# Where the operands of TensorE begin in SBUF: all tiles on multiples of 256 bytes, and some weights up to 252 bytes behind that

## The chip, the cores and the metric

The kernel runs on one core of one Trainium2 chip. The metric is the device time of one execution in microseconds, as the median of several runs. Lower is better. The profile is of one execution of the same program.

## The reference

One layer of a hybrid encoder block on 1024 tokens with a model width of 1024, in float32:

```
h = x + 0.5 * SwiGLU_1(RMSNorm(x))                      # D_FF = 2816
u = RMSNorm(h);  [q|k|v|g_ret|p|gates] = u @ w_in       # 7 x 1024 columns
ret  = retention(rotary(q), rotary(k), v)  (4 heads, chunks of 64), head norm, * silu(g_ret)
pool = multiscale_pool(p)  (windows 2, 4, 8, 16), per-group matrix, scale
h = h + (sigmoid(gate_0) * (ret @ w_ret_up) + sigmoid(gate_1) * (pool @ w_pool_up)) @ w_out
h = h + 0.5 * SwiGLU_2(RMSNorm(h))
out = RMSNorm(h)
```

## The kernel before, in words

**Arithmetic.** Every float32 operand of a matrix product is split into a high part, rounded by ScalarE to the type `F32R`, and a low part, the rest, which VectorE subtracts (`split`, lines 150 to 152). One product of a 128x128 block of weights with a moving operand of 512 (or 256) columns is three matmuls, issued by `mm3` (lines 169 to 173): high weights by high operand (L171), high weights by low operand (L172), low weights by high operand (L173). Each matmul brings its own load of 128x128 weights, which the profile shows under PEld.

**Tiles.** A tile of weights (`wt`, tag `wt`, 5 buffers) holds four blocks of 128 columns, first the high and then the low parts: 4096 bytes in each partition, so that a block is 512 bytes. A tile of a moving operand (`mv`, 28 buffers) holds 512 columns high and 512 low: also 4096 bytes. The other kinds are `t4` (results and some operands, 9 buffers), `raw` (weights as they come from memory, 4), `tl` (4) and `c2` (512 columns in one part, 2048 bytes, 8 buffers).

**Products.** `strassen` makes a pair of output tiles from seven products, each of four blocks, so twelve matmuls of 512 columns, with weights that `prep_w` makes by `weights(t[n], ...)`. Two such groups that share operands take some of their products a level deeper: `common` makes seven products of 256 columns, two blocks each, so 42 matmuls, from four tiles of weights (`wx`, `ws12`, `ws34`, `wy`). There are 43 calls of `common`, in both SwiGLU input stages and in the projection. The output stages of the two SwiGLUs are in `ffn_out`: there a `step` loads a tile of weights and one moving operand, and makes twelve matmuls of 512 columns; 77 steps in the first SwiGLU and 66 in the second, whose last product (`near`, `far`) is written another way round. Moving operands of the 256-column products are halves of `mv` tiles, or differences that `Next.blocks` puts into buffers of tag `tl` or `t4`.

**Order.** The order of the instructions on each engine is written out by the kernel: `Flow.run` issues the preparation of a step four steps ahead of its matmuls, and puts pieces of other work between (`flow.rate` pieces a step).

**Where tiles begin.** Tiles lie one behind the other in each partition. Ahead of them stand 1152 bytes of the program's own, then `vec` and `neg` (256 each), `cst` (1344), `warm` (which takes 32), `zero` (1024) and `ones_r` (512): the tiles of tags `t4` and `raw` begin at byte 4576 and follow each other by 4096 bytes. 4576 is 17 x 256 + 224, so all of these lie 224 bytes behind a multiple of 256. Then come two tiles of 32 bytes (tag `ss`), so that `wt`, `mv`, `tl` and `c2`, which follow, all begin 32 bytes behind a multiple of 256. A block of weights (512 bytes), a low part (2048 bytes) and a half of an operand (1024 bytes) begin at whole multiples of 256 from the start of their tile. So the operands of nearly all matmuls begin 32 bytes behind a multiple of 256, both the weights and the moving operand; the exceptions are those where one of the two is a tile of tag `t4`, 224 bytes behind it: in retention, the masked scores `sm` as weights (`inner`, output `ob`) and the state as moving operand (`across`, output `xb`); in the SwiGLU input stages, two of the three differences of R22 (`y3`, `y4`) as moving operands.

Of the kernel before, what the change touches and what calls it, by code (L numbers as in the profile page):

```python
# [3 lines left out]

# [1 line left out]

# [4 lines left out]
F32 = mybir.dt.float32  # L11
F32R = mybir.dt.float32r
BF16 = mybir.dt.bfloat16
# [4 lines left out]
P = 128  # L18
S = 1024
D = 1024  # L20
KT = D // P
H = S // 2
# [24 lines left out]
LOG_DECAY = np.log(1.0 - 2.0 ** (-5.0 - np.arange(NH, dtype=np.float64)))  # L47

N_PS, N_SUM, N_IDLE = 6, 2, 6
N_MV, N_T4, N_RAW, N_WT, N_TL, N_C2 = 28, 9, 4, 5, 4, 8  # L50
LOOK = 4

# [37 lines left out]
def block_kernel(ctx: ExitStack, tc, x, x_tok, vecs, f1_in, f1_out, w_in, w_v, pool_w, w_ret, w_pool, w_o,  # L90
# [5 lines left out]
    act = nc.scalar.activation  # L96
    copy = nc.scalar.copy
    soon = tc.high_priority
    flow = Flow()

    cp = ctx.enter_context(tc.tile_pool(name="cp", bufs=1))
    sb = ctx.enter_context(tc.tile_pool(name="sb", bufs=1))
# [4 lines left out]
    def mv(name):  # L107
        return sb.tile([P, 2, H], F32R, tag="mv", bufs=N_MV, name=name)

    def wt(name):  # L110
        return sb.tile([P, 2, 4, P], F32R, tag="wt", bufs=N_WT, name=name)


    def raw(name):
# [7 lines left out]

    def c2(name):
        return sb.tile([P, H], F32, tag="c2", bufs=N_C2, name=name)

    def bank(name):
        return ps.tile([P, H], F32, tag="ps", name=name)

    def sum_bank(name):

        return ps.tile([P, H], F32, tag="sum", bufs=N_SUM, name=name)

    def load(dst, src):
        nc.sync.dma_start(dst, src)
# [7 lines left out]
    LO, HI = slice(0, HD), slice(HD, H)  # L142
# [4 lines left out]
    def flat(w, j, n=4):  # L147
        return w[:, j, :n].rearrange("p a b -> p (a b)")

    def split(hi, lo, src):  # L150
        copy(hi, src)
        tt(lo, src, hi.bitcast(F32), SUB)  # L152
# [5 lines left out]
    def operand(src, name):  # L158
        m = mv(name)
        split(m[:, 0], m[:, 1], src)  # L160
        return m

    def weights(src, name):
        w = wt(name)
        n = src.shape[-1] // P
        split(flat(w, 0, n), flat(w, 1, n), src)
        return w

    def mm3(dst, w, m, start, stop):

        mm(dst, w[0], m[0], start=start, stop=False, skip_group_check=True)  # L171
        mm(dst, w[0], m[1], start=False, stop=False, skip_group_check=True)  # L172
        mm(dst, w[1], m[0], start=False, stop=stop, skip_group_check=True)  # L173

    def parts(m, at=slice(None)):
        return m[:, 0, at], m[:, 1, at]
# [7 lines left out]
    nc.vector.memset(warm, 1.0)  # L184
    act(warm, warm, AF.Square)
    nc.vector.tensor_scalar(neg, vec, -1.0, None, MUL)
    zero = cp.tile([P, H], BF16, name="zero")
    nc.vector.memset(zero, 0.0)
    for n in range(N_SUM):
        b = sum_bank(f"set{n}")  # L190
# [2 lines left out]
            mm(b, zero[:, :P], zero, start=True, stop=True)  # L193
    ident, ones = cst[:, C_ID : C_ID + P], cst[:, C_ONE : C_ONE + P]
    ones_r = cp.tile([P, P], F32R, name="ones_r")


    def inverse_root(sums, n, name):
# [322 lines left out]
    def common(nx, A, B, n):  # L521

        src, to, which, R = ("L12", "a", (0, 0), "R21") if n == 2 else ("S4", "b", (0, 1), "R22")
        w, t, a, b = {}, {}, A.t, B.t

        def prep1():
            w["x"] = weights(a[src], f"{A.name}wx{n}")
            s = t["s"] = c2(f"{A.name}s12{n}")
            tt(s[:, LO], b[src][:, LO], b[src][:, HI], ADD)
            tt(s[:, HI], s[:, LO], a[src][:, LO], SUB)  # L530
            w["s12"] = weights(s, f"{A.name}ws12{n}")

        def prep2():

            s = a[src] if n == 3 else c2(f"{A.name}s34{n}")
            tt(s[:, LO], a[src][:, LO], b[src][:, LO], SUB)
            tt(s[:, HI], a[src][:, HI], t["s"][:, HI], SUB)
            w["s34"] = weights(s, f"{A.name}ws34{n}")

        def prep3():  # L540
            w["y"] = weights(b[src][:, HI], f"{A.name}wy{n}")

        def prod(dst, k, at, m, start=False):
            for z in range(2):
                mm3(dst, parts(w[k], at + z), nx.block(R, m, z), start and z == 0, z == 1)


        def one():
            x, y = (bank(f"{A.name}{k}{n}") for k in "xy")
            t["x"], t["A"], t["B"] = x, A.dest(which), B.dest(which)  # L550
            prod(x[:, LO], "x", 0, (0, 0), True)
            with soon():
                copy(t["A"][:, LO], x[:, LO])
            prod(y[:, HI], "s12", 0, "y1", True)
            with soon():
                copy(t["B"][:, HI], y[:, HI])
            prod(a[to][:, LO], "x", 2, (1, 0))

        def two():
            x = t["x"]  # L560
            prod(x[:, LO], "s12", 2, "y2")
            with soon():
                tt(t["A"][:, HI], x[:, LO], t["B"][:, HI], ADD)
            prod(a[to][:, HI], "s34", 2, (1, 1))
            with soon():
                A.finish[n]()

        def three():
            x = t["x"]
            prod(b[to][:, LO], "y", 0, "y4")  # L570
            prod(x[:, LO], "s34", 0, "y3")
            with soon():
                copy(t["B"][:, LO], x[:, LO])
                tt(t["B"][:, HI], x[:, LO], t["B"][:, HI], ADD)
                B.finish[n]()

        return [(prep1, one), (prep2, two), (prep3, three)]


# [215 lines left out]
    def ffn_out(ops, ready, w, res, name, sink, end, last=None):  # L795
# [67 lines left out]
        def step(n, f, k, where, start, after):  # L863
            o = {}

            def prep():
                L, X = f(k)
                o["w"] = weights(L, f"{name}{n}w{k}")
                o["m"] = operand(X, f"{name}{n}m{k}")

            def body():
                if start and k == 0:
                    for i in range(4):
                        bk[where, i] = (sum_bank if where == "b" and i < N_SUM else bank)(f"{name}{n}{where}{i}")
                for i in range(4):
                    mm3(bk[where, i], parts(o["w"], i), parts(o["m"]), start and k == 0, k == FH - 1)
                    if k == FH - 1:
                        after(i)

            return prep, body  # L880
# [65 lines left out]
        L, X = {}, {}  # L946
# [55 lines left out]
    load(cst, consts)  # L1002
    flow.add(lambda: copy(ones_r, ones))
    first.work(first.r11, first.r21, first.r12, first.r22, first.p22, first.t2, first.t3, first.t1, first.t4_)
    x_sums = sb.tile([P, 8], F32, tag="ss", bufs=2, name="x_sums")

    def x_square(t):
        r = tl(f"xs{t}")
# [351 lines left out]
    class Unit:  # L1360
# [5 lines left out]
        def loads(self):  # L1366
            await_stored(f"q{self.h}", f"k{self.h}", f"v{self.name}")
            at = slice(self.nh * H, (self.nh + 1) * H)
            self.src = {}
            r = self.src["v"] = tl(f"v{self.name}")  # L1370
            load(r, vs[self.h // 2 * 2 + self.nh][:, self.h % 2 * S : (self.h % 2 + 1) * S])
            for n, spilled in (("q", qs), ("k", ks)):
                r = self.src[n] = tl(f"{n}{self.name}")
                for i in range(2):
                    load(half(r, i), spilled[2 * self.h + i][:, at])
            if self.nh == 0:
                self.dec = sb.tile([P, H], F32, tag="dec", bufs=1, name=f"dec{self.h}")
                load(self.dec, decay[self.h])
                self.ss = sb.tile([P, 8], F32, tag="ss", bufs=2, name=f"ss{self.h}")
                self.O = {}  # L1380

        def follow(self, u):
# [188 lines left out]
    def after(nx):  # L1571

        def t2(i):
            nx.r22(i)
            nx.t2(i)

        return {0: nx.r11, 4: nx.r21, 1: t2, 3: nx.t3, 2: nx.t1, 6: nx.t4_, 5: nx.p22}
# [83 lines left out]
    class Last(Norm):  # L1661
# [15 lines left out]
        def turned(self, acc):  # L1677


            def gains():  # L1680
                self.row = sb.tile([P, S], F32, tag="mv", bufs=N_MV, name=f"{self.name}row")
                load(self.row, g_row)
                self.ssq_e = sb.tile([P, 8], F32, tag="ss", bufs=2, name=f"{self.name}sse")

            def done(n):

                o = self.rows[n] = sb.tile([P, S], F32, tag="mv", bufs=N_MV, name=f"{self.name}o{n}")
                b = self.turn([acc[mt] for mt in range(4)], n)
                act(half(o, 1), b, AF.Square, accum_out=self.ssq_e[:, n : n + 1])
                tt(half(o, 0), b, half(self.row, 0), MUL)  # L1690
                v = self.sums[n] = sb.tile([P, 8], F32, tag="st", bufs=10, name=f"{self.name}e{n}")[:, :1]
                nc.vector.tensor_scalar(v, self.ssq_e[:, n : n + 1], 1.0 / D, EPS, MUL, ADD)

            def rest(n):

                b = self.turn([acc[mt] for mt in range(4, 8)], n)
                if n < N_SUM:
                    self.banks[n] = sum_bank(f"{self.name}s{n}")
                    copy(self.banks[n], b)
                else:  # L1700
                    copy(half(self.rows[n], 1), b)

            return gains, *(lambda f=f, n=n: f(n) for n in range(4) for f in (done, rest))
# [144 lines left out]
```

## Time and profile before

| what | value |
|---|---|
| runs before | 2163.72, 2163.72, 2165.25 us; median 2163.72 us |
| profiled execution, first to last instruction | 2160.9 us |
| TensorE matmul busy | 2148.0 us, 10668 matmuls |
| weight loads busy | 1816.9 us |
| VectorE busy | 1870.0 us |
| ScalarE busy | 1088.9 us |
| granted TensorE clock | 0.999 of full speed |

The profiled execution's span is 2160.9 us, 2.8 us under the median of the timed runs; what lies between is around the first and the last instruction. A matmul's end is modelled in these records, and matmuls overlap: what one costs in a stream is the distance from its start to the start of the next, which the view of the work in order of time shows.

By the starts of the matmuls in the trace the span falls into these stages: the first SwiGLU's input products to about 430 us and its output products to about 640 us, projections and values to about 1170 us, retention and the pooling branch to about 1370 us, the merge and the output projection to about 1520 us, the second SwiGLU's input products to about 1940 us and its output products to the end.

### The profile page before, as it was taken

To read this page: it belongs to the slowest core of one execution; us is meant where nothing else is said; L and a number is where in the kernel's file an instruction comes from. 1 tells how busy PE (TensorE), PEld (TensorE's weight loads), DVE (VectorE), ACT (ScalarE), POOL (GpSimd) and SP (SyncE) were. 2 spreads that over 40 slices of the span, in tenths; PEclk is the share of its full clock that TensorE was granted. 3 is DMA by queue.
4 is the path that set the end of the run, shared out by engine and by line. 5 is a ranking of instruction groups with operands and counts; after the bars stand their busy time and mean duration, and the time that the engine had idled before them with its cause. 6 is when DMAs were issued, how large, how long until landed. Compare 5 with 4: busy or idle time off the path is not lost.

```text
span 2160.9 us, 29697 instructions
## 1 busy us (share of the span) xinstructions
PE 2148.0 (99%) x10668; PEld 1816.9 (84%) x10668; DVE 1870.0 (87%) x3300; ACT 1088.9 (50%) x2047; POOL 0.2 (0%) x4
## 2 busy tenths in 40 slices
PE   9999999999999999999999999999999999999998
PEld 7888888888888888888888898887888888888887
DVE  8799899998788798899767877899999989999784
ACT  8544444545656444444426754446644444455463
POOL 0000000000000000000000000000000000000000
PEclk9999999999999999999999999999999999999999
DMA  7232323596323333333485567624133232359532
GB/s 261 69 129 104 101 93 127 165 339 207 122 93 107 109 127 108 118 107 119 153 268 191 167 224 256 218 97 160 65 117 103 98 107 99 118 185 334 178 122 78
DMA packets 117828, 320.92 MB, mean 149 GB/s; under 512 B 12976, under 2 KB 17200, under 8 KB 117680
## 3 DMA queue, kind: packets, MB, share of 16 engines
q1 hardware_dynamic: 117104, 317.97, 43.4%
q8 instruction: 83, 1.36, 0.3%
q10 hardware_dynamic: 576, 1.05, 0.1%
q14 instruction: 65, 0.53, 0.1%
HBM read 228.27 MB, written 90.70 MB: 148 GB/s over the span
## 4 chain that ended last, share of the span: by engine, by line
PE 90%; DVE 7%; ACT 1%; issue 1%; DMA 1%; SPq 0%; ACTq 0%; DVEq 0%
PE c_b L171 2%; PE c_b L173 2%; PE c_b L172 2%; PE a_b L173 2%; PE a_b L171 2%; PE a_b L172 2%; PE c_e L173 2%; PE c_e L171 2%; PE c_e L172 2%; PE a_e L173 2%; PE a_e L171 1%; PE a_e L172 1%; PE bp6b L172 1%; PE bp6b L173 1%; PE bp6b L171 1%; PE c_a L172 1%
## 5 line engine op out<-in xcount | busy, mean ns | idle before, releaser
L172 PE MATMUL c_b<-n3T,c_wS 128*128 128x512 f32 x176 | 68.5, 389 | 0.0
L173 PE MATMUL c_b<-n3T,c_wS 128*128 128x512 f32 x176 | 68.5, 389 | 0.0
L171 PE MATMUL c_b<-n3T,c_wS 128*128 128x512 f32 x176 | 68.2, 390 | 0.0
L171 PE MATMUL a_b<-n1T,a_wS 128*128 128x512 f32 x168 | 65.5, 390 | 0.0
L172 PE MATMUL a_b<-n1T,a_wS 128*128 128x512 f32 x168 | 65.4, 389 | 0.0
L173 PE MATMUL a_b<-n1T,a_wS 128*128 128x512 f32 x168 | 65.4, 389 | 0.0
L173 PE MATMUL a_a<-n1R,a_wL 128*128 128x512 f32 x120 | 46.7, 390 | 0.8 <-DVE a_wL L152 0.8
L171 PE MATMUL a_a<-n1R,a_wL 128*128 128x512 f32 x120 | 46.8, 390 | 0.0
L172 PE MATMUL a_a<-n1R,a_wL 128*128 128x512 f32 x120 | 46.7, 389 | 0.0
L172 PE MATMUL c_a<-n3R,c_wL 128*128 128x512 f32 x112 | 43.7, 390 | 0.0
L171 PE MATMUL c_a<-n3R,c_wL 128*128 128x512 f32 x112 | 43.6, 389 | 0.0
L173 PE MATMUL c_a<-n3R,c_wL 128*128 128x512 f32 x112 | 43.6, 389 | 0.0
L173 PEld LDWEIGHTS c_b<-n3T,c_wS 128*128 128x128 f32 x176 | 33.0, 188 | 6.9
L171 PEld LDWEIGHTS c_b<-n3T,c_wS 128*128 128x128 f32 x176 | 33.0, 188 | 6.9
L172 PEld LDWEIGHTS c_b<-n3T,c_wS 128*128 128x128 f32 x176 | 33.0, 188 | 6.8
L171 PEld LDWEIGHTS a_b<-n1T,a_wS 128*128 128x128 f32 x168 | 31.5, 188 | 6.8 <-ACT a_v L471 0.3
L173 PEld LDWEIGHTS a_b<-n1T,a_wS 128*128 128x128 f32 x168 | 31.5, 188 | 6.6
L172 PEld LDWEIGHTS a_b<-n1T,a_wS 128*128 128x128 f32 x168 | 31.5, 188 | 6.5
L173 PE MATMUL c_e<-n3T,c_wS 128*128 128x512 f32 x88 | 35.1, 399 | 0.4 <-DVE c_wS L152 0.4
L171 PE MATMUL c_e<-n3T,c_wS 128*128 128x512 f32 x88 | 34.5, 393 | 0.0
L172 PE MATMUL c_e<-n3T,c_wS 128*128 128x512 f32 x88 | 34.4, 391 | 0.0
L173 PE MATMUL a_e<-n1T,a_wS 128*128 128x512 f32 x84 | 33.4, 398 | 0.9 <-DVE a_wS L152 0.9
(3058 smaller groups left out, 8076.2 us busy)
## 6 DMA issues: line engine op xcount, KB each, us to landing
c_ra<-in_f_in SPq DMA_DIRECT2D x22, 512.0 KB, 3.6
c_rb<-in_f_in SPq DMA_DIRECT2D x22, 512.0 KB, 4.1
a_ra<-in_f_in SPq DMA_DIRECT2D x21, 512.0 KB, 3.6
a_rb<-in_f_in SPq DMA_DIRECT2D x21, 512.0 KB, 4.4
t<-au SPq DMA_DIRECT2D x11, 512.0 KB, 2.6
b<-ag SPq DMA_DIRECT2D x11, 512.0 KB, 2.7
r<-au SPq DMA_DIRECT2D x11, 512.0 KB, 3.6
br<-r SPq DMA_DIRECT2D x11, 512.0 KB, 5.4
```

Source lines behind the costliest of these rows:

```text
L171: mm(dst, w[0], m[0], start=start, stop=False, skip_group_check=True)
L172: mm(dst, w[0], m[1], start=False, stop=False, skip_group_check=True)
L173: mm(dst, w[1], m[0], start=False, stop=stop, skip_group_check=True)
```

## The change

The instructions of each engine, their order and their waits stay as they are. What changes is where tiles begin. The tile `zero`, which the first twelve matmuls read, takes a buffer of tag `c2` and no longer room of its own, a tile of 32 bytes called `line` is put behind `ones_r`, and tiles of tag `ss` take 128 bytes: tags `c2`, `t4`, `raw`, `wt`, `mv` and `tl` now all begin on multiples of 256 bytes. A tile of weights is 256 bytes longer, and a caller of `weights` can put the weights `at` floats behind its start. Two callers do: `common`, where all four tiles of a call have the same place, and `step` in `ffn_out`. One running count `places` numbers the calls of both; the place is the count times 22 (in `common`) or 23 (in `ffn_out`), modulo 64, in floats: 0 to 252 bytes. All other weights keep place 0.

```diff
+LINE = 64
...
-    flow = Flow()
+    flow, places = Flow(), count()
...
-    def wt(name):
-        return sb.tile([P, 2, 4, P], F32R, tag="wt", bufs=N_WT, name=name)
+    def wt(name, at=0):
+        w = sb.tile([P, S + LINE], F32R, tag="wt", bufs=N_WT, name=name)
+        return w[:, at : at + S].rearrange("p (z i c) -> p z i c", z=2, i=4)
...
+    def eights(name):
+        return sb.tile([P, 32], F32, tag="ss", bufs=2, name=name)[:, :8]
...
-    def weights(src, name):
-        w = wt(name)
+    def weights(src, name, at=0):
+        w = wt(name, at)
...
-    zero = cp.tile([P, H], BF16, name="zero")
+    zero = sb.tile([P, 2 * H], BF16, tag="c2", bufs=N_C2, name="zero")[:, :H]
...
+    cp.tile([P, 8], F32, name="line")
...
     def common(nx, A, B, n):
...
+        at = next(places) * 22 % LINE
...
-            w["x"] = weights(a[src], f"{A.name}wx{n}")
+            w["x"] = weights(a[src], f"{A.name}wx{n}", at)
...
-            w["s12"] = weights(s, f"{A.name}ws12{n}")
+            w["s12"] = weights(s, f"{A.name}ws12{n}", at)
...
-            w["s34"] = weights(s, f"{A.name}ws34{n}")
+            w["s34"] = weights(s, f"{A.name}ws34{n}", at)
...
-            w["y"] = weights(b[src][:, HI], f"{A.name}wy{n}")
+            w["y"] = weights(b[src][:, HI], f"{A.name}wy{n}", at)
...
     def step(n, f, k, where, start, after):
...
-                o["w"] = weights(L, f"{name}{n}w{k}")
+                o["w"] = weights(L, f"{name}{n}w{k}", next(places) * 23 % LINE)
```

In the 1716 matmuls of the `ffn_out` steps about a quarter each of the weights begin in the first, second, third and fourth 64 bytes behind a multiple of 256. In the 1806 matmuls of `common` it is 546 in the first 64 bytes and 1260 in the other three.

More of the change, by code (lines that the diff above doesn't have):

```diff
@@ L2 @@
 from contextlib import ExitStack, contextmanager
-from itertools import chain
+from itertools import chain, count
 import numpy as np
@@ L1004, in block_kernel @@
     first.work(first.r11, first.r21, first.r12, first.r22, first.p22, first.t2, first.t3, first.t1, first.t4_)
-    x_sums = sb.tile([P, 8], F32, tag="ss", bufs=2, name="x_sums")
+    x_sums = eights("x_sums")
     def x_square(t):
@@ L1378, in loads @@
                 load(self.dec, decay[self.h])
-                self.ss = sb.tile([P, 8], F32, tag="ss", bufs=2, name=f"ss{self.h}")
+                self.ss = eights(f"ss{self.h}")
                 self.O = {}
@@ L1682, in gains @@
                 load(self.row, g_row)
-                self.ssq_e = sb.tile([P, 8], F32, tag="ss", bufs=2, name=f"{self.name}sse")
+                self.ssq_e = eights(f"{self.name}sse")
             def done(n):
```

## The prediction

> **What bounds the kernel now.** I read the page first: span, busy times and the chain of work that ended last.
>
> ```profile
> span 2160.9 us, 29697 instructions
> ...
> PE 2148.0 (99%) x10668; PEld 1816.9 (84%) x10668; DVE 1870.0 (87%) x3300; ACT 1088.9 (50%) x2047; POOL 0.2 (0%) x4
> ...
> PE 90%; DVE 7%; ACT 1%; issue 1%; DMA 1%; SPq 0%; ACTq 0%; DVEq 0%
> ```
>
> TensorE is busy for 99% of the span and makes 90% of the chain. So the time is the number of matmuls times their distance, and a change to where operands lie can matter only through that distance, or by making another engine late. Next I read the work in order of time, for the distance of matmuls of 512 columns, in a stretch where nothing waits (eleven rows, the first and the last shown), and for when a weight load starts beside them.
>
> ```profile
> 519.70 0.39 PE L172 MATMUL bp6b<-bp7m,bp7w 128*128 128x512 f32 x1
> ...
> 521.96 0.39 PE L173 MATMUL bp6b<-bp7m,bp7w 128*128 128x512 f32 x1
> ...
> 1520.00 0.39 PE L171 MATMUL wo3b<-mgR,wo3wS 128*128 128x512 f32 x1
> 1520.01 0.19 PEld L172 LDWEIGHTS wo3b<-mgR,wo3wS 128*128 128x128 f32 x1
> ```
>
> Ten steps take 2.26 us: about 226 ns each. The load of the next weights starts 0.01 us after a matmul starts, so both streams of reads begin together each time. The same view where retention goes from `st` to `ob`, matmuls of 256 columns:
>
> ```profile
> 1225.06 0.28 PE L172 MATMUL st<-v,kd 128*128 128x256 f32 x1
> ...
> 1225.66 0.28 PE L171 MATMUL ob<-v,sm 128*128 128x256 f32 x1
> ...
> 1226.00 0.28 PE L171 MATMUL ob<-v,sm 128*128 128x256 f32 x1
> ```
>
> Five steps of `st` take 0.60 us, 120 ns each; three of `ob` take 0.34 us, 113.3 ns each. These are the same kind of instruction on the same shape. What differs is the place: `st` has weights and moving operand both 32 bytes behind a multiple of 256, `ob` has weights of tag `t4`, at 224. The groups by line and shape repeat it (mean duration, which is the distance plus 163 ns in both cases):
>
> ```profile
> L172 PE MATMUL c_b<-n3T,c_wS 128*128 128x512 f32 x176 | 68.5, 389 | 0.0
> ...
> L172 PE MATMUL st<-v,kd 128*128 128x256 f32 x48 | 13.6, 283 | 0.0
> ...
> L172 PE MATMUL ob<-v,sm 128*128 128x256 f32 x48 | 13.2, 276 | 0.0
> ...
> L173 PE MATMUL c_x<-n3R22y,c_ws 128*128 128x256 f32 x40 | 11.2, 280 | 0.0
> ...
> L173 PE MATMUL c_x<-n3R21y,c_ws 128*128 128x256 f32 x32 | 9.1, 283 | 0.0
> ...
> L1505 PE MATMUL ot<-cst,o 128*128 128x128 f32 x64 | 7.6, 273 | 0.0
> ```
>
> Where both begin at 32 the duration is 283 (`st`, and `c_x` with R21's differences in `tl`); where one lies in `t4` it is 276 (`ob`), and it is 280 for `c_x` with R22, half of whose operands lie in `t4` and half in `tl`. So there is a price of about 6.7 ns a matmul for beginning at the same place modulo 256, and it is in the kernel's steady state: 389 less 163 is 226 for 512 columns.
>
> **How a distance is made up.** 512 columns take 226.7 and 256 take 120.0: 106.7 ns for 256 columns, and 13.3 ns beside them. In `ob` it is 6.7 beside them. 13.3 is twice 6.7, and 6.7 ns is what 16 columns take, 64 bytes of a partition. My reading: operands are read in pieces of 64 bytes. 512 floats that begin at 32 modulo 64 touch 33 pieces and not 32, one piece (6.7 ns) too many; 224 is 32 modulo 64 too, so `ob` has that too. And where the load of weights begins in the same 64 bytes of 256, both want the same part of the memory at once, and the matmul waits for one more piece. The first half of the reading is an inference; the second is what the rows show.
>
> **The change part by part.** Program counts: 8042 matmuls of 512 columns and 2334 of 256 in F32R, of 10668 records.
>
> (a) 6326 matmuls of 512 columns end with both operands at 0. Bounds: no gain (only the relative place counts, and it stays equal), and 13.3 ns (both parts go), below nothing too, see the rivals. I take 6.7, the piece that alignment takes away, since the collision of equal starts stays: 6326 x 6.7 = 42.2 us.
>
> (b) 1716 matmuls of the `ffn_out` steps. Three quarters (1287) begin in other 64 bytes than the operand: 6.7 to 13.3, taken at 10.0, since weights at odd places were not seen to be free: 12.9. The other quarter as in (a): 2.9. Together 15.7 us.
>
> (c) 1806 matmuls of `common`. In the two windows below the 42 of a call take 4.97 and 5.03 us, 119 ns each. After it 113.3 (the `ob` row) is the dear end; the cheap end is bound by the loads of weights, which in the transposes `ot` are what 128 columns wait for (duration 273, so 110 by the same 163). I take 112: 7 x 1806 = 12.7 us.
>
> (d) Retention: `st` and the scores, 240 of 256 columns, lose a piece, 1.6 us; `ob`, and `xb` like it, win a piece and get a collision, nothing.
>
> ```profile
> 125.00:500.00 375.00, 372.82 (x1919) 318.25 (x1920) 352.19 (x630) 179.01 (x327) 0.00 (x0) 1.00 0.44 149
> 1420.00:1500.00 80.00, 78.98 (x345) 64.24 (x344) 78.25 (x130) 46.94 (x83) 0.00 (x0) 1.00 0.39 132
> 1500.00:1920.00 420.00, 419.55 (x2188) 359.66 (x2188) 395.27 (x723) 209.50 (x389) 0.00 (x0) 1.00 0.31 107
> 1661.28:1666.31 5.03, 5.03 (x43) 5.03 (x42) 3.97 (x7) 3.12 (x6) 0.00 (x0) 1.00 0.66 201
> 1671.78:1676.75 4.97, 4.97 (x43) 4.96 (x42) 4.97 (x11) 3.04 (x6) 0.00 (x0) 1.00 0.02 3
> ...
> L152 DVE TENSOR_TENSOR c_wS<-c_S,c_wS 128x512 fp32r<-128x512 f32 x46 | 31.4, 685 | 1.2 <-ACT c_wS L151 1.2
> ...
> 1520.27 0.69 DVE L1629 TENSOR_TENSOR wo<-wo2b,wo 128x512 f32<-128x512 f32 x1
> 1520.87 0.69 DVE L257 TENSOR_TENSOR n3ssq<-n3ssq,n3q 128x512 f32<-128x512 f32 x1
> ```
>
> (e) What comes late next. The windows (columns: length, then busy time of PE, PEld, DVE, ACT, POOL) show VectorE at 352 of 375, 78 of 80 and 395 of 420 us in the stages with Strassen products. Those 4452 matmuls save about 30 us, which leaves VectorE 10 us of slack in each long stage and none at 1420 to 1500. It has more than busy time tells, since one operation shows 685 ns but the next starts 0.60 us after it. I let VectorE take back a third of the 30 us: 10 us. If it took all, 30.
>
> (f) Costed at nothing: writing weights at odd places, 143 tiles in `ffn_out` and 172 in `common`, two operations each, off TensorE's path while VectorE and ScalarE have slack; the VectorE rows at 32 and 224 are alike, but no row is at a place that is no multiple of 32. 630 operations dearer by one piece would be 4 us, hidden except in (e)'s stages. `zero` in a `c2` buffer adds no wait: its matmuls are over in the first 7 us. DMA is 1% of the chain.
>
> Sum: 42.2 + 15.7 + 12.7 + 1.6 - 10 = 62.2 us. The profiled execution's span is 2160.9 us; the median of the runs, 2163.7, is 2.8 more, which stays: 2098.7 and 2.8 are 2101.5, so 2101 us.
>
> **The rivals.**
>
> *Only the relative place counts.* The fixed 6.7 ns is not a piece too many but a cost of every such matmul. For it: no row here has a moving F32R operand on a multiple of 64. Then (a) is nothing; (b) 1287 x 6.7 = 8.6; (c) 546 at 120 and 1260 at about 115 (between `ob` and `c_x` with R22) against 119 now, 4.5; `ob` loses 144 x 6.7 = 1.0. 2163.7 - 12.1 = 2152 us.
>
> *The collision goes with the alignment.* With whole pieces the two streams interleave. For it: 13.3 is all there is to win. 8042 x 13.3 = 107 and 2334 x 10 = 23, of which VectorE takes back 30 or so, since its windows then bind: 100 less, 2064 us. The Trainium skill, "TensorE: Matmul & The Clock Gate", section "Back-to-back issue gap", has N / 2.4 + 2.5 ns for a warm matmul, 216 for 512 columns; the 226 here differ, and going by the page the gain would be 10.9 and not 13.3 ns on the 8042, an estimate near 2083.
>
> *Nothing moves.* Distances are set by something that goes with tags and not with addresses. Against it: `c_x` shows both durations for the same product with its operand in `t4` or `tl`. Time 2164 us. By the Trainium skill, the same page, section "Step-by-step: what each phase is for", TensorE has two independent read ports and loading the next weights takes nothing from the running matmul's reads; that would make this rival certain, and the rows `st` and `ob` disagree with it by 6.7 ns.
>
> *Slower: equal starts on whole pieces collide more.* At 32 the first piece of either stream is half used, which sets them apart after the first meeting; on 256 they would meet again at later pieces, in all 6326 matmuls of (a). The trace has dearer matmuls of the same shape and place, up to 397 against 389:
>
> ```profile
> L173 PE MATMUL c_b<-n3T,c_wS x176: 387/389/397, 1534.3 to 1928.6; 128*128 128x512 f32 x176
> ```
>
> At 8 ns each that is 51 us, with the rest unmoved: 2214 us. It decides from 4.6 ns a matmul on, where it eats up (b) and (c) with 28 us. Against it: the 226 are steady, a fixed price and not repeated ones.
>
> **How the numbers follow.** Forecast (equal starts collide, alignment saves one piece) 0.50, own range 2085 to 2125 by (b) and (e); relative place alone 0.12 (2152); collision gone 0.12 (2064); nothing moves 0.08 (2164); slower 0.18 (2168 to 2214). The range from 2064 to 2168 leaves out the slower case. A difference of 0.2%, 4.3 us, is about what a measurement of this kernel can tell from none. Faster by more: 0.50 + 0.12 + 0.12 = 0.74; within it 0.08; slower 0.18.
>
> **What would show it right or wrong.** Right: the group `c_b` with `c_wS` at 382 and not 389, `bp` and `dp` groups at 376 to 382, `st` at 276, `ob` unmoved at 276, `common` groups at 273 to 276; VectorE's share up to about 89%, with longer idle times of TensorE before `c_e` and `a_e` products. Wrong: `c_b` at 389 (relative place alone, if `bp` falls; nothing, if not), at 376 (collision gone), or at 393 and more (slower).

## The result, and the profile after

The changed kernel takes 2174.78 us (median; 2173.60 to 2174.82), the kernel before 2163.72 us beside it. The ratio is 1.0048, with a 95% interval from 1.0032 to 1.0064: slower, by about 11 us. The forecast was 2101 us, with a range from 2064 to 2168, so the time lies outside it and on the other side.

The page of the changed kernel, its span, busy times and the chain of work that ended last:

```profile
span 2171.8 us, 29697 instructions
...
PE 2158.6 (99%) x10668; PEld 1817.3 (84%) x10668; DVE 1871.4 (86%) x3300; ACT 1090.0 (50%) x2047; POOL 0.2 (0%) x4
...
PE 90%; DVE 7%; DMA 1%; ACT 1%; issue 1%; SPq 0%; ACTq 0%; DVEq 0%
```

The number of instructions is the same, and the span and TensorE's busy time grew by almost the same: 10.9 and 10.6 us. The chain is what it was. No new wait holds the kernel up; the matmuls themselves stand further apart. Which ones, the groups by line and shape tell; first the changed kernel (count, then busy us and mean ns of one, then idle time before them):

```profile
L179 PE MATMUL c_b<-n3T,c_wS 128*128 128x512 f32 x176 | 68.5, 389 | 0.0
...
L179 PE MATMUL bp6b<-bp7m,bp7w 128*128 128x512 f32 x44 | 17.4, 394 | 0.0
L179 PE MATMUL dp6b<-dp6m,dp6w 128*128 128x512 f32 x44 | 17.4, 396 | 0.0
...
L179 PE MATMUL ob<-v,sm 128*128 128x256 f32 x48 | 13.6, 283 | 0.0
L179 PE MATMUL st<-v,kd 128*128 128x256 f32 x48 | 13.6, 283 | 0.0
...
L179 PE MATMUL c_x<-n3R22y,c_ws 128*128 128x256 f32 x40 | 11.3, 282 | 0.0
L179 PE MATMUL c_x<-n3R,c_wx 128*128 128x256 f32 x36 | 10.1, 281 | 0.0
```

The same view of the kernel before, for the groups that the prediction did not quote:

```profile
L172 PE MATMUL bp6b<-bp7m,bp7w 128*128 128x512 f32 x44 | 17.1, 389 | 0.0
L172 PE MATMUL dp6b<-dp6m,dp6w 128*128 128x512 f32 x44 | 17.1, 389 | 0.0
...
L172 PE MATMUL xb<-state,q 128*128 128x256 f32 x48 | 13.6, 283 | 0.5 <-DVE state L152 0.5
...
L171 PE MATMUL xb<-state,q 128*128 128x256 f32 x48 | 13.5, 282 | 0.3 <-DVE rg L1506 0.3
L173 PE MATMUL xb<-state,q 128*128 128x256 f32 x48 | 13.4, 279 | 0.0
...
L172 PE MATMUL c_x<-n3R,c_wx 128*128 128x256 f32 x36 | 10.2, 283 | 0.0
```

The reader sees three things. `c_b`, for the 6326 matmuls of 512 columns that now have both operands on a multiple of 256, stays at 389 ns. The `ffn_out` groups (`bp...` in the first SwiGLU, `dp...` in the second), whose weights now begin anywhere behind it, rise from 389 to 394 and 396. Of the 256-column groups `ob` rises from 276 to 283, `st` stays, and `common` (`c_x` with `c_wx`) falls by 2 ns. The work in order of time, changed kernel, shows the `ffn_out` matmuls directly (eleven of them, first and last):

```profile
519.11 0.39 PE L179 MATMUL bp1a<-bp2m,bp2w 128*128 128x512 f32 x1
...
521.42 0.39 PE L180 MATMUL bp1a<-bp2m,bp2w 128*128 128x512 f32 x1
```

Ten steps take 2.31 us where they took 2.26. And the windows of one stretch of 200 us within that stage (columns as in the prediction; the count in brackets is what to read), before:

```profile
433.00:633.00 200.00, 200.00 (x884) 165.62 (x883) 163.45 (x265) 103.61 (x180) 0.00 (x0) 1.00 0.60 199
```

and after:

```profile
433.00:633.00 200.00, 200.00 (x861) 161.61 (x860) 159.41 (x257) 101.40 (x176) 0.00 (x0) 1.00 0.59 195
```

TensorE is busy throughout in both, at the full granted clock, and makes 23 matmuls fewer: 226.2 ns became 232.3.

Where the 10.9 us are, worked out from the starts of all matmuls in the two traces: `ffn_out` of the first SwiGLU 209.4 to 214.9 us, of the second 194.9 to 199.5 (together +10.1); `ob` and `xb` +1.1; all other matmuls of 512 columns 1431.2 to 1431.8 (+0.6); `common` 219.1 to 218.6 (-0.5). That makes 11.3, and what is left (-0.4) is spread over the rest.

Below, a *distance* is from the start of one matmul to the start of the next. A distance of a group leaves out the few that a wait stretched (over 262 ns for 512 columns, over 140 for 256). A *place* of weights is the number of bytes from the moving operand's start to the weights' start, modulo 256, where nothing else is said.

### The profile page after: what moved, and what is told of

Its sections match the earlier page's. It is cut to its first block, busy times and chain, and to the rows that moved or that the text cites. A ratio compares the mean times of both kernels' runs of the same rounds, so it can differ in the third digit from the quotient of the medians.

```text
span 2171.8 us, 29697 instructions
## 1 busy us (share of the span) xinstructions
PE 2158.6 (99%) x10668; PEld 1817.3 (84%) x10668; DVE 1871.4 (86%) x3300; ACT 1090.0 (50%) x2047; POOL 0.2 (0%) x4
## 4 chain that ended last, share of the span: by engine, by line
PE 90%; DVE 7%; DMA 1%; ACT 1%; issue 1%; SPq 0%; ACTq 0%; DVEq 0%
PE c_b L178 2%; PE c_b L180 2%; PE c_b L179 2%; PE a_b L180 2%; PE a_b L178 2%; PE a_b L179 2%; PE c_e L180 2%; PE c_e L178 2%; PE c_e L179 2%; PE a_e L180 1%; PE bp6b L178 1%; PE bp6b L180 1%; PE bp6b L179 1%; PE a_e L179 1%; PE a_e L178 1%; PE c_a L179 1%
## 5 line engine op out<-in xcount | busy, mean ns | idle before, releaser
L178 PE MATMUL c_b<-n3T,c_wS 128*128 128x512 f32 x176 | 68.2, 390 | 0.0
L178 PE MATMUL a_b<-n1T,a_wS 128*128 128x512 f32 x168 | 65.4, 389 | 0.0
L178 PE MATMUL a_a<-n1R,a_wL 128*128 128x512 f32 x120 | 46.8, 390 | 0.0
L178 PE MATMUL c_a<-n3R,c_wL 128*128 128x512 f32 x112 | 43.6, 389 | 0.0
L178 PEld LDWEIGHTS c_b<-n3T,c_wS 128*128 128x128 f32 x176 | 33.0, 188 | 6.8
L178 PEld LDWEIGHTS a_b<-n1T,a_wS 128*128 128x128 f32 x168 | 31.5, 188 | 6.7
L178 PE MATMUL c_e<-n3T,c_wS 128*128 128x512 f32 x88 | 34.5, 392 | 0.0
L179 PE MATMUL c_e<-n3T,c_wL 128*128 128x512 f32 x88 | 34.3, 390 | 0.0
```

## The experiments

The theory formed on the result: a distance has no part for alignment; equal places are the cheap state for 512 columns, and most unequal ones cost a 6.7 ns step more. The rivals are the recorded reading (pieces of 64 bytes, with the collision lower where places differ), and that the added 10 us come from something beside the matmuls' own operands (writing weights to odd places, the longer tiles, the order). Three of the runs split the change, three measure matmuls alone, four put weights at one fixed place.

### Streams of matmuls alone, by place (e1_scan)

Streams of 36 matmuls in F32R, each with its own weights, as in `mm3`. In `at` the weights are displaced, in `by` the moving operand, in `eq` both; the number is in bytes.

```diff
+    for n in (512, 256, 128):
+        for at in [*range(64), 64, 128]:
+            done = stream(f"at{4 * at}b{n}c", at, 0, n)
+        for by in (1, 8, 16, 22, 32, 48):
+            done = stream(f"by{4 * by}b{n}c", 0, by, n)
+            done = stream(f"eq{4 * by}b{n}c", by, by, n)
```

> This kernel does none of the block's work: it loads one piece of x, and then runs streams of 36 matmuls with nothing else on the chip, in the pattern of the change's products (each with a load of its own, four blocks of weights, high and low part). Only the places differ: at4b512 has weights 4 bytes behind a multiple of 256 and the moving operand on it, by4b512 the other way round, eq4b512 both at 4. Theory A (only the relative place modulo 256 counts): at0, at256, at512 and every eq stand at 227 ns for 512 columns, all other at and by at 229 to 236; for 256 columns 120 where the places are equal and 114 to 121 elsewhere. Theory B (a place that is no multiple of 16 or 64 bytes costs by itself): at64, at128, at192 stand like at0, and eq4, eq88 stand as dear as at4, at88. Theory C (the prices in the block come from writes of VectorE and ScalarE beside the matmuls): all streams of one width stand alike here.

The groups of single tiles of this run (shortest, median and longest ns; then the first and the last start in us):

```profile
L43 PE MATMUL at0b512c<-m,w x36: 389/389/397, 18.0 to 26.0; 128*128 128x512 f32 x36
L43 PE MATMUL at64b512c<-m,w x36: 388/394/398, 151.7 to 159.9; 128*128 128x512 f32 x36
L43 PE MATMUL at120b512c<-m,w x36: 389/389/395, 269.1 to 277.0; 128*128 128x512 f32 x36
L43 PE MATMUL eq4b512c<-m,w x36: 392/400/402, 577.5 to 585.8; 128*128 128x512 f32 x36
L43 PE MATMUL eq64b512c<-m,w x36: 388/389/397, 610.8 to 618.8; 128*128 128x512 f32 x36
L43 PE MATMUL eq88b512c<-m,w x36: 390/396/401, 627.3 to 635.5; 128*128 128x512 f32 x36
...
L43 PE MATMUL at0b256c<-m,w x36: 278/283/283, 668.9 to 673.1; 128*128 128x256 f32 x36
L43 PE MATMUL at88b256c<-m,w x36: 276/276/281, 762.1 to 766.1; 128*128 128x256 f32 x36
```

512 columns at place 0 show the kernel's 389; at 64 it is 394; both operands at 64 (`eq64`) are 389 again. Of the 64 places in steps of 4 bytes, taking means over the last 25 distances of a stream, seven have 226.7 ns (0, 120, 132, 144, 156, 204, 252), and the other 57 have 228.4 to 237.4; 30 of them are within half a nanosecond of 233.3, one step of 6.7 more. That is a mean: at 64 the single distances alternate between 231 and 235 or 236. Displacing weights by 256 or 512 bytes is as good as by 0 (226.7). For 256 columns it is the reverse: equal places have 120.0, and most others have less, 113.4 at 52, 64, 76, 88 and 192. At 128 columns every place has about 111.7.

Theory A has a miss here. It had every `eq` at 227; that holds at 32, 64, 128 and 192 (226.6 to 226.7), but not at 4 (237.8) and 88 (233.6), where the moving operand does not begin on a multiple of 32 bytes. So that the relative place alone decides is shown for moving operands on multiples of 32, where those of the kernel before and of the changed one lie, and not beyond. Theory B had these two `eq` as dear as `at4` and `at88` (232.3 and 233.3), and so they are, or dearer; its other half, 64, 128 and 192 as cheap as 0, is refuted (233.2, 233.5 and 228.9).

The mean of the 64 places is 232.0 ns for 512 columns, and the `ffn_out` groups of the changed kernel, which run through the places, have 232.5 in the first SwiGLU and 232.2 in the second (65 undisplaced matmuls among 857). The mean of the places that are multiples of 8 bytes, which `common` runs through, is 118.0 for 256 columns, and `common` has 118.3. So the price of the change is that of its matmuls' places, and needs nothing else. Theory C, prices that come from writes beside the matmuls, falls too: the places differ here, and no such writes run beside the streams.

### The change with all places 0, and its two parts (e2_align, e3_ffn_only, e4_common_only)

e2 keeps the alignment and takes both displacements away:

```diff
-        at = next(places) * 22 % LINE
+        at = 0
...
-                o["w"] = weights(L, f"{name}{n}w{k}", next(places) * 23 % LINE)
+                o["w"] = weights(L, f"{name}{n}w{k}")
```

e3 sets only `common` to 0, so only `ffn_out` is displaced; e4 sets only `ffn_out` to 0, so only `common` is. Both keep the running count going, so what stays displaced has the places of the change.

> The change without any place: all tiles on multiples of 256 bytes, all weights at 0. Theory A: relative places as before in all products of 512 columns and in common, equal in ob and xb, which were unequal: 1.0 + 0.5 us more than before, so 2165 us. The prediction's piece too many: 2164 - 42 - 11 or more, about 2105. A theory in which the alignment itself is what cost the time: 2170 and more.

> The change with places in the ffn_out steps alone (the same places as there), weights of common at 0. Theory A: 1716 matmuls at 232.4 and not 226.7, so 10 us on e2_align: 2175. If the dear part of the change lay in common: as e2_align.

> The change with places in common alone (the same places as there), those of the ffn_out steps at 0. Theory A: 1806 matmuls at 118.3 and not 119.8, so 2 to 3 us under e2_align: 2162 to 2163. If any unequal place were dear in itself: 2170 and more.

| | median us | kernel before, same chip | ratio, 95% interval |
|---|---|---|---|
| e2, alignment alone | 2165.90 | 2164.93 | 1.0006 (0.9997 to 1.0015) |
| e3, displaced in `ffn_out` | 2176.70 | 2164.93 | 1.0057 (1.0043 to 1.0070) |
| e4, displaced in `common` | 2163.77 | 2164.93 | 0.9998 (0.9989 to 1.0007) |

The chain of work that ended last in e2, and its groups by line and shape:

```profile
PE 91%; DVE 6%; ACT 1%; issue 1%; DMA 0%; SPq 0%; DVEq 0%; ACTq 0%
```

```profile
L179 PE MATMUL c_b<-n3T,c_wS 128*128 128x512 f32 x176 | 68.5, 389 | 0.0
...
L179 PE MATMUL ob<-v,sm 128*128 128x256 f32 x48 | 13.6, 283 | 0.0
...
L179 PE MATMUL c_x<-n3R22y,c_ws 128*128 128x256 f32 x40 | 11.3, 283 | 0.0
```

Alignment alone gives `c_b` nothing. It costs `ob` its 7 ns and `c_x` with R22 3 ns, because `t4` now begins at the same place as the rest: the two groups lose an unequal place that they had by accident. e3 has the whole loss; in its windows of the stretch shown above

```profile
433.00:633.00 200.00, 200.00 (x862) 161.60 (x861) 159.38 (x257) 101.82 (x177) 0.00 (x0) 1.00 0.58 198
```

there are 862 matmuls, as in the changed kernel (861), while e2 has 884, as before:

```profile
433.00:633.00 200.00, 200.00 (x884) 165.64 (x884) 163.46 (x265) 104.23 (x181) 0.00 (x0) 1.00 0.59 200
```

In e4 the group of `common`

```profile
L179 PE MATMUL c_x<-n3R,c_wx 128*128 128x256 f32 x36 | 10.1, 281 | 0.0
```

falls by 2 ns from 283, and e4's time can't be told from the kernel before. The three together say: loss from `ffn_out`, next to nothing from alignment, and a small gain from `common`, which the distances show (119.8 ns in e2, 118.3 in e4) and the medians alone, 2.1 us apart with overlapping intervals, would not settle. That the longer tiles or `zero` in a `c2` buffer cost something falls with e2, which has them.

### All weights at one place (e7_all64, e8_all120)

The default place of `weights` becomes 16 floats (64 bytes) in e7 and 30 floats (120 bytes) in e8, and both callers use it; so all weights that `weights` makes are displaced.

```diff
+AT = 16
...
-    def weights(src, name, at=0):
+    def weights(src, name, at=AT):
...
-        at = next(places) * 22 % LINE
+        at = AT
...
-                o["w"] = weights(L, f"{name}{n}w{k}", next(places) * 23 % LINE)
+                o["w"] = weights(L, f"{name}{n}w{k}", AT)
```

> One place, 64 bytes, for all weights that the function weights makes. Theory A2 by the first scan (233.3 at 64, 226.7 at 0): 7560 matmuls of 512 columns dearer by 6.6 ns, 50 us, and common 10.5 us cheaper: 2205 us. If the price comes from the places changing from tile to tile, and one place for all is as good as another: 2155.

> As e7_all64 with 120 bytes, one of the six unequal places that the first scan has at 226.7 for 512 columns (and 119.2 for 256). Theory A2: as e2_align, 2166 us, 2 more for the products of v, whose moving operand is a tile of weights. If every unequal place, or every place that is no multiple of 16, costs in the kernel: 2205 or more.

e7 takes 2204.29 us beside 2163.73 (1.0185, from 1.0171 to 1.0199), e8 2167.41 beside 2163.73 (1.0015, from 1.0006 to 1.0024). A place that was dear in the scan (64) and one that was cheap (120) are so in the whole kernel too. Page of e7, and behind it its groups:

```profile
PE 2191.2 (99%) x10668; PEld 1814.8 (82%) x10668; DVE 1878.2 (85%) x3300; ACT 1089.5 (49%) x2047; POOL 0.2 (0%) x4
```

```profile
L180 PE MATMUL c_b<-n3T,c_wS 128*128 128x512 f32 x176 | 69.6, 395 | 0.0
...
L180 PE MATMUL bp6b<-bp7m,bp7w 128*128 128x512 f32 x44 | 17.4, 396 | 0.0
```

and of e8:

```profile
L180 PE MATMUL c_b<-n3T,c_wS 128*128 128x512 f32 x176 | 68.5, 389 | 0.0
```

By the starts, the 512-column matmuls of e7 outside `ffn_out` take 1466.8 us, 35 more than in the changed kernel, at 233.0 ns; those of `ffn_out` 233.3 and 232.8. Beside e2 that is 46 us more in all 8042, of which `common`, at 115.5 ns and not 119.8, gives back 6.5 (220.5 to 214.0 us with its waits): 39.5 us, and the spans of e7 and e2 are 39.8 apart. That the expectation's 2205 us came out is in part luck: it had 50 and 10.5 us for these two terms, and both were 4 too large. In e8 the same matmuls are at 227.3 and 226.7.

### Which operand, which part, which type (e5_scan2)

Streams alone again. `m..w..` gives the moving operand and the weights places of their own in steps of 32 bytes; `ml` displaces only the moving operand's low part, `wl` the weights' low part, `bl` each block of weights, `mw` both low parts; `hat` is the same stream in bf16.

```diff
+    for d in (4, 8, 16, 24, 32, 40, 48, 56):
+        done = stream(f"ml{4 * d}b512c", 0, 0, 512, mlo=d)
+        done = stream(f"wl{4 * d}b512c", 0, 0, 512, wlo=d)
+        done = stream(f"bl{4 * d}b512c", 0, 0, 512, block=d)
+        done = stream(f"mw{4 * d}b512c", 0, 0, 512, mlo=d, wlo=d)
+    for by in range(0, 64, 8):
+        for at in range(0, 64, 8):
+            done = stream(f"m{4 * by}w{4 * at}b512c", at, by, 512)
...
+    for at in (0, 1, 8, 16, 32, 48, 64):
+        done = stream(f"hat{2 * at}b512c", at, 0, 512, of=(wh, mh))
```

> Streams of matmuls alone again, none of the block's work. ml: the low part of the moving operand lies so many bytes off, wl: the low part of the weights, bl: each block of weights from the block ahead, mw: both low parts; m..w..: moving operand and weights at these places, in steps of 32 bytes; hat: bf16 operands at 0 and with weights off. Theory A2 (two fixed patterns of the two read streams, 226.7 and 233.3 on the mean, chosen by the difference of places where the moving operand begins on a multiple of 32): m..w.. at 226.7 wherever m and w are equal, and 228 to 238 where they differ by 32, 64, 96, 128, 160, 192, 224 as in the first scan; no stream of 512 columns under 226. Theory D (a shorter pattern exists that the first scan did not meet): some stream at 220 or less. bf16: alike at all places if the patterns come from the reading of four bytes a column.

Single tiles of this run:

```profile
L48 PE MATMUL m0w0b512c<-m,w x36: 389/389/397, 287.9 to 295.8; 128*128 128x512 f32 x36
L48 PE MATMUL m0w32b512c<-m,w x36: 392/395/397, 296.0 to 304.2; 128*128 128x512 f32 x36
L48 PE MATMUL m32w0b512c<-m,w x36: 393/396/399, 354.7 to 362.8; 128*128 128x512 f32 x36
L48 PE MATMUL m32w32b512c<-m,w x36: 387/389/397, 363.1 to 371.0; 128*128 128x512 f32 x36
...
L48 PE MATMUL hat64b512c<-mh,wh x36: 379/379/379, 989.7 to 997.2; 128*128 128x512 bf16 x36
```

`m32w32`, where the kernel before stood, and `m0w0`, where the changed one stands, are both 389. All eight equal pairs have 226.6 to 226.7 ns, and the 56 unequal ones 228.8 to 234.4; the table repeats along its diagonals, so it is the difference modulo 256 that counts and not either operand's alignment, as long as the moving operand is on a multiple of 32. Displacing a part alone never helped: 228.9 to 233.6. No F32R stream of 512 columns is under 226.6, so theory D's shorter pattern did not show. At 256 columns the four equal pairs of this run have 120.0 and the 28 unequal ones 113.3 to 119.9.

In bf16 all seven places of the weights have 215.84 ns. That agrees with the 216 for 512 columns that the Trainium skill gives in "TensorE: Matmul & The Clock Gate", section "Back-to-back issue gap", for an isolated matmul; the 131 ns that the section has for a sustained stream of loads and matmuls is not what these streams show. The 226.7 of the F32R stream, and its steps by place, are then a matter of F32R matmuls and not of the streams' form.

### Widths, and where a stream comes from (e9_scan3)

Moving operands of 512 to 192 columns, weights of 128 to 32 columns, and streams of 256 columns entered from other streams: of 512 columns with equal places (`p`), of 256 (`q`), of 128 (`r`), of 512 at the same place (`s`), or with the moving operand at 64 (`t`).

```diff
+    for n in (512, 448, 384, 320, 256, 192):
+        for at in (0, 16, 24, 64):
+            done = stream(f"at{at}b{n}c", at // 4, 0, n)
+    for cols in (128, 96, 64, 32):
+        for at in (0, 16, 64):
+            done = stream(f"k{cols}at{at}b512c", at // 4, 0, 512, cols)
+    for at in (64, 88, 52, 76, 120):
+        for e, first in (("p", (0, 0, 512)), ("q", (0, 0, 256)), ("r", (0, 0, 128)), ("s", (at // 4, 0, 512)),
+                         ("t", (0, 16, 512))):
+            stream(f"e{at}{e}z", *first)
+            done = stream(f"from{at}{e}b256c", at // 4, 0, 256)
```

> Streams of matmuls alone. First the number of columns of the moving operand (512 to 192) at equal places and at 16, 24 and 64 bytes, then the number of columns of the weights (k128 to k32) with 512 moving columns, then matmuls of 256 columns at five unequal places, each entered from five other streams (from64p and so on). What is open: the prediction took the 13.3 ns beside 106.7 per 256 columns for one piece too many of the operand and one collision. Theory F (the load's own reads take the moving operand's time, the same sum wherever it fits): 13.3 at equal places for every number of columns, and with narrower weights less, in proportion: 10, 6.7, 3.3 for 96, 64, 32. Theory G (a fixed restart of every F32R matmul, two pieces): 13.3 for narrow weights too. For the entries: if a stream can settle in more than one pattern at the same places, from64 has both 113.3 and 117.8, by its entry; if the place alone sets it, one value for each place.

```profile
L42 PE MATMUL k32at0b512c<-m,w x36: 388/392/398, 235.5 to 243.6; 128*32 128x512 f32 x36
L42 PE MATMUL from64pb256c<-m,w x36: 280/281/282, 268.6 to 272.8; 128*128 128x256 f32 x36
L42 PE MATMUL from64tb256c<-m,w x36: 276/276/285, 310.3 to 314.3; 128*128 128x256 f32 x36
```

At equal places the distance is 226.6 for 512 columns, 202.7 for 448, 173.3 for 384, 146.7 for 320 and 120.0 for 256. Four of these five are the columns' own time (106.7 ns for 256) and 13.3, the fifth 16.0. So 13.3 is a fixed part at four of the widths, though not at every one; 192 columns have 111.9, nearly the 111.7 of 128 columns in the first scan. Narrower weights do not lower the distance: at equal places 96, 64 and 32 columns have 230.1, 230.2 and 231.7, against 226.7 for 128. Theory F, a cost in proportion to the weight load, is refuted. Theory G had 13.3 for narrow weights too, and they have 16.7 to 18.4; so a fixed restart is not shown either. With weights of 32 columns the places 0, 16 and 64 are alike at 231.7.

The last two lines are the same instructions at the same place, 64, and settle at 281 or 276 (117.8 or 113.4 ns) by what ran before them. At 88, four of five entries give 113.4 and one 116.8; at 76 all five give 113.4. A stream finds a repeating pattern, and which one depends on its entry at 64, 88 and 52. A place of 512 columns showed two values as well: at 16 bytes the first scan had 233.3 and this one 226.7.

### Common's weights at one place (e6_common64, e10_common88)

The scans made 64 and 88 the cheap places for 256 columns. Both kernels leave `ffn_out` at 0:

```diff
-        at = next(places) * 22 % LINE
+        at = 16      # e6; 22 in e10
...
-                o["w"] = weights(L, f"{name}{n}w{k}", next(places) * 23 % LINE)
+                o["w"] = weights(L, f"{name}{n}w{k}")
```

> The change with one place for all weights of common, 64 bytes, and 0 in the ffn_out steps. The first scan has 113.4 ns for 256 columns there and 120.0 at equal places. Theory A2: 1806 matmuls, 119.2 to 113.4, 10.5 us under e2_align: 2155 us, under the kernel before by 0.4%. If what the places do to matmuls of 256 columns is lost again in the SwiGLU input stages because VectorE is late: 2160 to 2165.

> The change with one place for all weights of common, 88 bytes (113.4 in the first scan, and 114.1 in the two calls of the changed kernel that have it), and 0 in the ffn_out steps. If this place keeps its pattern after any entry: 1806 matmuls from 119.8 to 114.2, 10 us under e2_align, 2155 us, faster than both kernels by 0.4%. If it is lost like at 64 bytes: 2163.

e6 takes 2163.62 us beside 2163.73 (0.9997, from 0.9988 to 1.0005); its `common` is at 117.8 ns and not at the 113.4 of the first scan. That miss led to the entries of e9: `common` comes from 512-column matmuls with equal places, entry `p`, where 64 gives 117.8. The time lies where the expectation had put a late VectorE, but the distance is the reason. The entry as scanned does not settle everything: e7's `common` follows matmuls at its own place, entry `s`, which has 113.4 in e9, and shows 115.5. e10 takes 2160.06 beside 2163.85: 0.9984, from 0.9975 to 0.9993, the one version that is below both kernels, and between the expectation's two cases. Groups of `common` in e6

```profile
L179 PE MATMUL c_x<-n3R,c_wx 128*128 128x256 f32 x36 | 10.1, 280 | 0.0
```

and in e10:

```profile
L179 PE MATMUL c_y<-n3R,c_ws 128*128 128x256 f32 x36 | 9.9, 276 | 0.0
...
L178 PE MATMUL c_x<-n3R21y,c_ws 128*128 128x256 f32 x32 | 9.2, 287 | 0.0
L179 PE MATMUL c_x<-n3R21y,c_ws 128*128 128x256 f32 x32 | 8.9, 278 | 0.0
```

The chain of e10:

```profile
PE 87%; DVE 10%; issue 1%; ACT 1%; DMA 1%; SPq 0%; DVEq 0%; ACTq 0%
```

The largest of TensorE's waits in e10 (us in total, times, longest):

```profile
PE a_x L178 <- DVE ag L573: 1.6, 2, 1.0
```

Here the saving is seen being taken back in part. `common` is at 114.2 ns against 119.8 in e2: 1806 times 5.6 is 10.1 us. The spans are 4.5 us apart (2159.1 and 2163.6). VectorE's share of the chain rises from 6% in e2 to 10%, the wait for `ag`, which VectorE makes, is the largest (e2's list of waits has none for `a_x`), and the first matmuls of a product with R21's differences (L178, 287) are 9 ns longer than those behind them (278). By the starts, `common` with its waits takes 213.6 us and not 220.5, so 3.2 of the 10.1 come back in itself, and the other matmuls of 512 columns take 1434.5 and not 1432.1, which is 2.4 more. What is left, 4.5, is the difference of the spans. That VectorE is what takes the rest back is read from the chain and the waits; no run made VectorE faster to show it.

## Why the prediction was wrong

**What bounds the kernel** was right: no wait decides the result, and TensorE's busy time grew by 10.6 us where the span grew by 10.9.

**"How a distance is made up" is the step that failed.** Its inference, that 32 modulo 64 touches one piece of 64 bytes too many, was taken from the number alone: 6.7 ns is what 16 columns take. The equal pairs of e5 refute it: 32 and 32, 0 and 0, 64 and 64 are all 226.7. Its other half, called what the rows show, was two things: a price of 6.7 ns at equal places, which rows of 256 columns did show, and a cause, both streams wanting the same part of the memory, which none showed. The price was carried over to 512 columns, of which no row had unequal places: 226 was taken to contain it. There the sign is the other one: 226.7 equal, mostly 233.3 unequal.

**(a)** 42.2 us forecast, nothing measured: `c_b` at 389, in the changed kernel and in e2, and +0.6 us in all 512-column matmuls outside the displaced steps. This is the largest term, and with it the forecast fell.

**(b)** 15.7 us forecast as a gain, 10.1 measured as a loss: 1716 matmuls not 9.2 ns nearer but 5.9 ns further apart. The bounds given for unequal places, 6.7 to 13.3 of gain, came from the 256-column rows and did not go below nothing, though those of (a) did.

**(c)** 12.7 us forecast (7 x 1806 is 12.6), 0.5 measured (with waits). The sign is right and the size wrong: 119.2 to 118.3 ns and not to 112. `ob` at 113.3 was read as what any unequal place costs, but `ob` stood at 192, one of five such places of 64. The kernel before held the warning: `xb`, the other group with one operand in `t4`, has weights 64 bytes behind its moving operand, and showed 282, 283 and 279 in the rows above, where `ob` showed 276. The first two of these rows have a wait in them; its starts give 116.3 ns as distance, between `ob` and the equal places. The prediction called it "like `ob`" and showed none of its rows.

**(d)** `st` was to fall and stayed; `ob` was to stay and rose by 6.6 ns, from 113.4 to 120.0: 1.0 us, as the rival "relative place" had it.

**(e)** could not act, since nothing was saved. In e10, which saves, about 5.6 of 10.1 us were taken back, more than the third that the sum had; the chain and the waits point to VectorE.

**(f)** holds: e3 and e4 write weights to the odd places, and the matmuls' distances account for their times. VectorE's own rows agree: writing the low part of `bp3w` (L152 before, L159 after) took 691 ns at the one place and 692 at the displaced ones:

```profile
L152 DVE TENSOR_TENSOR bp3w<-bs,bp3w 128x512 fp32r<-128x512 f32 x11 | 7.6, 691 | 11.7 <-ACT bp3w L151 11.7
...
L159 DVE TENSOR_TENSOR bp3w<-bs,bp3w 128x512 fp32r<-128x512 f32 x11 | 7.6, 692 | 12.5 <-ACT bp3w L158 12.5
```

**The rivals.** "Only the relative place counts" was right on (a) and `ob`, and on what counts for moving operands on multiples of 32; its 2152 us fell with the same carrying over of 256-column prices. "Slower" had the sign; its mechanism, equal starts on whole pieces colliding more, is refuted by `c_b` and e2. The loss sits where the starts are *un*equal. "The collision goes with the alignment" and "nothing moves" are refuted by e2 and e7. The two independent read ports that the Trainium skill states in "TensorE: Matmul & The Clock Gate", section "Step-by-step: what each phase is for", would make place indifferent; the F32R streams disagree by 6.7 ns, and the bf16 stream agrees at the seven places tried.

**What stays open.** What in the chip sets the patterns: why 120, 132, 144, 156, 204 and 252 are as cheap as 0 for 512 columns, why 256 columns are the other way round, and why the entry decides. That the load of weights takes part is likely, since the weights' place counts, but a stream without loads was not tried, and narrower loads do not make the stream faster (e9).

## What to carry to other kernels

A price read from one shape is a price of that shape: before it is carried over to another, find a row of that shape in the disputed state, and if none exists keep both signs in the bounds. Read every group that is in the state, not only the one that shows the effect best; here a second group (`xb`, 116.3 ns) already did not fit the first (`ob`, 113.4). For steady streams of F32R matmuls of 512 columns keep weights and moving operand at equal places modulo 256, and the moving operand on a multiple of 32 bytes; a displacement may pay at 256 columns, but only at single places, which have to be measured in their own surroundings, and only as far as the next engine follows.

## What the runs showed of the hardware

- F32R matmuls of 512 columns, each with its own weights: 226.7 ns when both operands begin at the same place modulo 256 bytes (and the moving operand on a multiple of 32), 228.4 to 237.4 at 57 of the 63 other differences in steps of 4, 226.7 at six (first scan). 256 columns: 120.0 at equal places, 113.4 to 123.4 at others. 128 columns: 111.7 at all.
- bf16 with the same form: 215.84 ns at all seven places of the weights tried.
- A moving operand off the multiples of 32 bytes can be dear even at equal places (512 columns): 4 bytes behind a multiple of 256 it has 238.1 ns with weights at 0 and 237.8 with weights at 4; 88 bytes behind it 231.2 and, with weights at 88, 233.6.
- Distances of such streams are multi-valued: the same place, 64, gave 117.8 or 113.4 ns for 256 columns by what ran before it.
